# A fused recurrent, retention and feed-forward block: in the gates, weight forms and retention operands are issued behind stated copies, and the last value stages take one PSUM tile per key block

## The chip, the core and the metric

The kernel runs on one core of a Trainium2 chip. The metric is device microseconds of one execution, as the median of several runs. The engines that matter here are TensorE (PE in the profile; its weight loads are PEld), VectorE (DVE), ScalarE (ACT) and SyncE (SP), which issues the loads. Each engine works its own queue in order.

## What is computed

One layer over 528 tokens (16 meta tokens and 512 of the sequence) with model width 1024. After an RMS norm, one large projection gives a recurrent branch (an RG-LRU with its gate, called branch a), a retention branch with four heads (branch b) and a gate for each branch. The two branches are mixed, projected and added; a gated convolutional feed-forward follows.

```python
z = xn @ w_in[l]
u_rnn, u_gate, q, k, v, g_ret, ga, gb = jnp.split(z, IN_SPLITS, axis=-1)
...
o_a = hr * jax.nn.gelu(u_gate)
...
o = retention(q, k, v.reshape(bsz, t, RET_HEADS, RET_DV))
o_b = head_rms(o).reshape(bsz, t, RET_HEADS * RET_DV) * jax.nn.silu(g_ret)
mixed = (jax.nn.sigmoid(ga) * (o_a @ w_branch_rnn[l])
         + jax.nn.sigmoid(gb) * (o_b @ w_branch_ret[l]))
h = h + mixed @ w_out[l]
```

## The kernel before

**Numbers.** Every fp32 matrix is split into a high and a low fp16 piece; a product is three fp16 matmuls (high by high, high by low, low by high). `split` (L91 to L93) makes the pieces: an activation on ScalarE writes the high one, an instruction on VectorE the low one, and reads the high one for it.

**Fast units.** A weight block that is marked `fast` is multiplied with seven half-size products in place of eight. For that the block is formed in five steps (`fast_steps`): B11; B21 with B22; the sums (three VectorE additions in place in the raw tile, L255 to L257); T1 with T3; T4 with T2. The last two steps read what the sums have written. The tokens' forms (A11, A12, F3, F5, F6, F7) are made once.

**Queue of steps.** Weights come by DMA into `raw`, two buffers of 1 MB, and are formed into `wt`, ten buffers. The steps of all units stand in one list in the order of use. `tick` emits the next step if the units in hand take no more than `ahead` tiles; `get` emits what remains of a unit when it is needed. From L716 on the order of the instructions on each engine is not written out by hand: a planner takes the program's order as priority, simulates the engines and issues what is ready, so a step that is late in the program can be issued early. `tc.issue_after(ins)` adds an edge from `ins` to each instruction of the block that runs on the engine of `ins`.

**Gates.** `fast_products` (L839) runs the seven products of a gate unit in the order P1, P7, P6, P2, P5, P3, P4, each of 12 matmuls of 257 columns. P1, P6, P5 and P3 add up in one PSUM bank, `pa`; between them ScalarE copies the bank out (`keep`, L852). P7 and P4 use `pe`, P2 uses `pb`. VectorE adds the kept copies (L869, L873, L880), ScalarE applies the gate's function (L885). `gated` runs the two gate units of a retention head between the output products of the next head (L932). At the end of a unit `ob_forms` makes the second branch's operands from the gated head: four subtractions on VectorE and four splits. `gate_a` takes the gates of branch a, with `branch` (60 matmuls, `pm`) between; the last head's gate units lie among them, and one `u_ga` unit is started before the retention gate ahead of it is finished. `gate_b` takes the gates of branch b and then `mix_products`, the second branch's own fast products, the only reader of the `ob` tiles.

**Values.** `values` (L887) makes the values of one head for five blocks of keys. Four blocks take 24 matmuls of 512 columns, the last 16. Two blocks share a PSUM tile of two banks (`acc`, two tiles in this stage), one bank each; a split follows each block. Heads 2 and 3 have their value stages between the gated heads, near 322 to 345 and 372 to 396 us.

**After the gates** come the output projection, the norm and the up products, where forms of the activations already wait in a list `pending` behind a last copy and a last sum.

## Time and profile before

| | before |
|---|---|
| median of 3 runs | 1069.34 us (1069.12 to 1069.63) |
| profiled execution, own time | 1069.46 us |
| its span | 1067.7 us |
| TensorE busy | 1050.2 us, 98% |
| VectorE busy | 860.5 us, 81% |
| ScalarE busy | 589.7 us, 55% |
| DMA | 111.49 MB, mean 104 GB/s |
| granted TensorE clock, mean | 0.999 |

The span is the stretch that the profiler saw; the own time has 1.8 us more around it. TensorE's busy time has little room above it, and matmuls overlap one another in the rows, so what can be won or lost lies in single gaps of TensorE. They are found in the time line by the idle time in brackets behind an instruction, with the one that ended it. The rows give start, length, engine, line and operation; where several equal instructions follow one another, they are one row with a count.

### The profile page before, as it was taken

To read this page: it belongs to the slowest core of one execution; us is meant where nothing else is said; L and a number is where in the kernel's file an instruction comes from. 1 tells how busy PE (TensorE), PEld (TensorE's weight loads), DVE (VectorE), ACT (ScalarE), POOL (GpSimd) and SP (SyncE) were. 2 spreads that over 40 slices of the span, in tenths; PEclk is the share of its full clock that TensorE was granted. 3 is DMA by queue.
4 is the path that set the end of the run, shared out by engine and by line. 5 is a ranking of instruction groups with operands and counts; after the bars stand their busy time and mean duration, and the time that the engine had idled before them with its cause. 6 is when DMAs were issued, how large, how long until landed. Compare 5 with 4: busy or idle time off the path is not lost.

```text
span 1067.7 us, 21013 instructions
## 1 busy us (share of the span) xinstructions
PE 1050.2 (98%) x8995; PEld 851.5 (80%) x8995; DVE 860.5 (81%) x1289; ACT 589.7 (55%) x927; POOL 6.9 (1%) x20
## 2 busy tenths in 40 slices
PE   9999999999999999999999999999999999999997
PEld 6888888865684848888888886588888888888884
DVE  6885799998786969887787785489789897988975
ACT  7568954434564747466454453475565465454442
POOL 2000000000000000000000000000000000000000
PEclk9999999999999999999999999999999999999999
DMA  8341243431211322333333365042332324214322
GB/s 255 102 133 44 80 139 119 160 120 40 80 41 51 108 65 65 122 95 106 118 105 119 103 214 178 7 153 86 113 107 92 119 81 133 66 60 137 102 80 80
DMA packets 108989, 111.49 MB, mean 104 GB/s; under 512 B 5610, under 2 KB 100560, under 8 KB 108896
## 3 DMA queue, kind: packets, MB, share of 16 engines
q1 hardware_dynamic: 108448, 109.74, 31.9%
q8 instruction: 70, 1.15, 0.4%
q10 hardware_dynamic: 160, 0.27, 0.1%
q0 software_dynamic: 288, 0.14, 0.1%
q14 instruction: 23, 0.19, 0.1%
HBM read 108.04 MB, written 2.10 MB: 103 GB/s over the span
## 4 chain that ended last, share of the span: by engine, by line
PE 74%; DVE 14%; ACT 8%; issue 2%; DMA 1%; ACTq 0%; DVEq 0%
PE ps L398 29%; PE P L1455 9%; PE pa L847 9%; PE pm L398 4%; PE ps L910 4%; DVE wt L93 4%; PE pe L847 4%; PE ps L1183 3%; PE pb L847 2%; PE ps L411 2%; PE pa L1346 2%; ACT wt L92 2%; PE ps L932 1%; DVE rnn L645 1%; PE pe L1346 1%
## 5 line engine op out<-in xcount | busy, mean ns | idle before, releaser
L398 PEld LDWEIGHTS <-wt 128*128 128x128 f16 x3840 | 373.2, 97 | 58.2 <-DVE t L739 1.4
L93 DVE SCALAR_TENSOR_TENSOR wt<-raw,wt 128x1024 f16<-128x1024 f32 (+2 forms) x278 | 303.9, 1105 | 68.9 <-ACT wt L92 67.9
L92 ACT ACTIVATE wt<-raw 128x1024 f16<-128x1024 f32 (+2 forms) x278 | 263.4, 963 | 153.5 <-PE P L1455 25.3
L847 PEld LDWEIGHTS <-wt 128*128 128x128 f16 x2016 | 195.1, 97 | 34.7 <-issue 7.4
L398 PE MATMUL ps<-x2h,wt 128*128 128x258 f16 x1184 | 181.2, 273 | 0.0
L398 PE MATMUL ps<-xh,wt 128*128 128x257 f16 (+2 forms) x1056 | 163.9, 275 | 1.1 <-DVE t L739 1.1
L398 PE MATMUL ps<-x2l,wt 128*128 128x258 f16 x592 | 113.2, 272 | 0.0
L398 PE MATMUL ps<-xl,wt 128*128 128x257 f16 (+2 forms) x528 | 102.2, 275 | 0.0
L1455 PE MATMUL P<-wt,act 128*128 128x256 f16 x792 | 88.3, 273 | 0.0
L1455 PEld LDWEIGHTS <-act 128*128 128x128 f16 x792 | 77.5, 98 | 9.0
L1324 DVE SCALAR_TENSOR_TENSOR cv<-ps,vt,cv 128x512 f32<-128x512 f32 x80 | 59.8, 747 | 26.5 <-ACT cv L1322 25.6
L910 PE MATMUL ps<-wt,xh 128*128 128x512 f16 x256 | 76.1, 379 | 2.3 <-DVE v L93 2.3
L847 PE MATMUL pa<-xs,wt 128*128 128x257 f16 x576 | 71.6, 273 | 3.4 <-ACT kept L852 3.1
L398 PE MATMUL pm<-oa,wt 128*128 128x257 f16 x480 | 55.4, 274 | 0.0
L1322 ACT ACTIVATE cv<-ps,vt,vt 128x512 f32<-128x512 f32 x40 | 31.0, 774 | 38.5 <-PE ps L398 37.9
L910 PEld LDWEIGHTS <-xh 128*128 128x128 f16 x256 | 24.8, 98 | 31.4 <-issue 3.4
L910 PE MATMUL ps<-wt,xl 128*128 128x512 f16 x128 | 48.3, 379 | 0.0
L255 DVE TENSOR_TENSOR raw<-raw 128x1024 f32<-128x1024 f32 x39 | 47.6, 1220 | 0.7
L847 PE MATMUL pa<-ob,wt 128*128 128x257 f16 x384 | 45.7, 274 | 0.6 <-ACT last L852 0.5
L1183 PE MATMUL ps<-wt,mx 128*128 128x512 f16 x192 | 44.3, 378 | 0.0
L1346 PEld LDWEIGHTS <-wt 128*128 128x128 f16 x336 | 32.6, 97 | 4.4
L411 PEld LDWEIGHTS <-wt 128*128 128x128 f16 x288 | 27.9, 97 | 5.8 <-issue 1.3
(290 smaller groups left out, 1406.6 us busy)
## 6 DMA issues: line engine op xcount, KB each, us to landing
raw<-in_w_in SPq DMA_DIRECT2D x40, 1024.0 KB, 4.9
raw<-in_w_up SPq DMA_DIRECT2D x24, 1024.0 KB, 5.2
raw<-in_w_down SPq DMA_DIRECT2D x48, 256.0 KB, 3.4
raw<-in_w_branch_ret SPq DMA_DIRECT2D x16, 512.0 KB, 4.8
raw<-in_w_branch_rnn SPq DMA_DIRECT2D x8, 640.0 KB, 4.5
raw<-in_w_out SPq DMA_DIRECT2D x4, 1024.0 KB, 5.1
xin<-in_x SPq DMA_DIRECT2D x4, 512.0 KB, 5.7
raw<-in_w_in SPq DMA_DIRECT2D x4, 512.0 KB, 8.2
```

Of the source, the lines that this page charges most:

```text
L92: nc.scalar.activation(hi, src, AF.Copy, scale=s)
L93: nc.vector.scalar_tensor_tensor(lo, src, s, hi, op0=ALU.mult, op1=ALU.subtract)
L255: nc.vector.tensor_tensor(pair, pair, rv[:, :, right].rearrange("p (h k) c -> p h k c", h=2), op=ALU.add)
L398: nc.tensor.matmul(ps[:, hf, :n], w(aw, k, col, P), src(ax, k, c0, n), start=k == 0 and (aw, ax) == (0, 0), stop=k == nk - 1 and aw == 1)
L411: mm = nc.tensor.matmul(ps[:, hf, :n], w(aw, k, col, P), src(ax, k, c0, n), start=k == 0 and (aw, ax) == (0, 0), stop=k == KD - 1 and aw == 1)
L847: nc.tensor.matmul(ps[:, :257], ws[k // 4](wf, aw, k % 4), src(xf_, ax, k), start=first and k == 0 and (aw, ax) == (0, 0), stop=k == last_ ...
L910: nc.tensor.matmul(pb, xf(ax, k, XF + j0, nb), w(aw, k % 4, 0, 512), start=i == 0, stop=i == 23)
L1183: nc.tensor.matmul(ps[:, n], mx[k][:, a, c0:c0 + P], wo[k // 2](aw, k % 2, n * 512, 512), start=k == 0 and (a, aw) == (0, 0), stop=k == ks ...
L1322: nc.scalar.activation(vv_, src[:, :, 2:258], AF.Identity, scale=vt2[:, 96 + ch:97 + ch], bias=bias)
L1324: nc.vector.scalar_tensor_tensor(vv_, src[:, :, j:j + 256], vt2[:, 48 * j + ch:48 * j + ch + 1], vv_, op0=ALU.mult, op1=ALU.add)
L1346: nc.tensor.matmul(ps[:, :258], w(wf, aw, k), x2_form(xf_, ax, k), start=first and k == 0 and (aw, ax) == (0, 0), stop=k == 3 and aw == 1, ...
L1455: nc.tensor.matmul(pd[:, 256 * tt:256 * tt + 256], t[:, ax, c0 + tt * P:c0 + tt * P + P], w(wf, aw, i), start=q % 6 == 0 and tt == 0 and i ...
```

## The change

In `fast_steps` the two steps that read the sums are wrapped, so that their instructions on ScalarE may not be issued before the gate copy (`keep`) that was traced last; they carry a mark `late`. `tick` can be told to leave late steps where they are, and the gates tell it so at P1 and P7. The operands of the second branch are no longer made at once at the end of a retention gate unit: `ob_forms` returns three portions, which are put in `pending` and emitted by `flush`, one at each of P7, P6 and P5 of a later gate unit or after a key block of `values`, also behind the last copy. `gating` switches the edge off inside `mix_products`. In `values`, heads 2 and 3 take a PSUM tile for each key block and use its first bank.

```diff
@@ -1,4 +1,4 @@
-from contextlib import ExitStack
+from contextlib import ExitStack, nullcontext
 
 import concourse.bass as bass
 import concourse.tile as tile
@@ -262,11 +262,25 @@
             i, c0 = at[nm]
             return tiles[i][a][:, k, c0:c0 + bc]
 
+        def late(run):
+            def behind():
+                with behind_copy():
+                    run()
+            behind.late = True
+            return behind
+
         wviews.append(form)
         return [cut(top, left), cut(low, slice(0, 2 * bc)), sums,
-                cut(top, slice(0, 2 * bc)), cut(low, slice(0, 2 * bc))]
+                late(cut(top, slice(0, 2 * bc))), late(cut(low, slice(0, 2 * bc)))]
 
     steps = []
+    last_keep = [None]
+    gating = [True]
+
+    def behind_copy():
+
+        return nullcontext() if last_keep[0] is None or not gating[0] else tc.issue_after(last_keep[0])
+
     done = [0]
     ahead = [6]
     current = [0]
@@ -292,7 +306,8 @@
             emit_step()
         return wviews[u]
 
-    def tick(n=1):
+    def tick(n=1, late=True):
+
 
         for _ in range(n):
             if done[0] == len(steps):
@@ -301,6 +316,8 @@
                 queue(unit_load())
             u = steps[done[0]][0]
             if sum(unit_tiles(i) for i in range(current[0], u + 1)) > ahead[0]:
+                return
+            if not late and hasattr(steps[done[0]][1], "late"):
                 return
             emit_step()
 
@@ -849,7 +866,7 @@
                                      skip_group_check=True)
 
         def keep(dst, ps):
-            nc.scalar.activation(dst, ps[:, :257], AF.Copy)
+            last_keep[0] = nc.scalar.activation(dst, ps[:, :257], AF.Copy).ins
 
         kept, last = wtile("kept"), wtile("last")
         g0, g1 = wtile("g0"), wtile("g1")
@@ -888,9 +905,9 @@
         vt = []
         wa, wb = get(u_v[h][0]), get(u_v[h][1])
         for b, (j0, nb) in enumerate(JB):
-            if b % 2 == 0:
+            if h >= 2 or b % 2 == 0:
                 ps = acc("ps")
-            pb = ps[:, b % 2]
+            pb = ps[:, 0 if h >= 2 else b % 2]
             vt.append(piece([P, 2, 512], F16, f"v{h}"))
             i = 0
             if b == 4:
@@ -910,6 +927,7 @@
                     nc.tensor.matmul(pb, xf(ax, k, XF + j0, nb), w(aw, k % 4, 0, 512), start=i == 0, stop=i == 23)
                     i += 1
             split(vt[b][:, 0], vt[b][:, 1], pb, S_V / (SW * S_XN))
+            flush()
             tick()
         vv[h] = vt
 
@@ -957,28 +975,57 @@
         def finish(j, g):
             nc.vector.tensor_mul(ot[2 * i + j], g[:, :TQ], ot[2 * i + j])
             if j == 0:
-                ob_forms(h, i, ot[2 * i], ot[2 * i + 1])
+                pending.extend(ob_forms(h, i, ot[2 * i], ot[2 * i + 1]))
 
         return fast_products([get(u_gr[h][i])], x_forms, gate_func(AF.Silu), finish)
 
     def ob_forms(h, i, t0, t1):
 
         h0, h1 = slice(0, 257), slice(257, TQ)
-        d, y = wtile("d"), wtile("y")
-        nc.vector.tensor_tensor(d[:, h1], t0[:, h1], t1[:, h1], op=ALU.subtract)
-        nc.vector.tensor_tensor(y[:, h0], t0[:, h0], t0[:, h1], op=ALU.subtract)
-        nc.vector.tensor_tensor(d[:, h0], t0[:, h0], d[:, h1], op=ALU.subtract)
-        nc.vector.tensor_tensor(y[:, h1], d[:, h0], t1[:, h0], op=ALU.subtract)
-        if i == 0:
-            ob_a11.append(piece([P, 2, TQ], F16, "ob11"))
-        a11 = ob_a11[h]
-        split(a11[:, 0, 257 * i:257 * i + 257], a11[:, 1, 257 * i:257 * i + 257], t0[:, h0], S_OB)
-        at = {"A11": (a11, 257 * i)}
-        for src, s, nms in ((t1, S_OB, ("A12", "A22")), (y, S_OB, ("F7", "F3")), (d, -S_OB, ("F6", "F5"))):
+        at = {}
+        tmp = {}
+        ob.append(at)
+
+        def differences():
+            d, y = tmp["d"], tmp["y"] = wtile("d"), wtile("y")
+            nc.vector.tensor_tensor(d[:, h1], t0[:, h1], t1[:, h1], op=ALU.subtract)
+            nc.vector.tensor_tensor(y[:, h0], t0[:, h0], t0[:, h1], op=ALU.subtract)
+            nc.vector.tensor_tensor(d[:, h0], t0[:, h0], d[:, h1], op=ALU.subtract)
+            nc.vector.tensor_tensor(y[:, h1], d[:, h0], t1[:, h0], op=ALU.subtract)
+
+        def both(src, s, nms):
             t = piece([P, 2, TQ], F16, "ob")
             split(t[:, 0], t[:, 1], src[:, :TQ], s)
             at.update({nm: (t, 257 * n) for n, nm in enumerate(nms)})
-        ob.append(at)
+
+        def plain():
+            if i == 0:
+                ob_a11.append(piece([P, 2, TQ], F16, "ob11"))
+            a11 = ob_a11[h]
+            split(a11[:, 0, 257 * i:257 * i + 257], a11[:, 1, 257 * i:257 * i + 257], t0[:, h0], S_OB)
+            at["A11"] = (a11, 257 * i)
+            both(t1, S_OB, ("A12", "A22"))
+
+        def formed():
+            both(tmp["y"], S_OB, ("F7", "F3"))
+            both(tmp["d"], -S_OB, ("F6", "F5"))
+
+        return [differences, plain, formed]
+
+    pending = []
+
+    def flush(n=1):
+
+        for _ in range(min(n, len(pending))):
+            with behind_copy():
+                pending.pop(0)()
+
+    def advance(run, *names):
+        for nm in names:
+            next(run)
+            if nm in ("P7", "P6", "P5"):
+                flush()
+            tick(1, nm not in ("P1", "P7"))
 
     def scale_head(h, i):
         for d in (2 * i, 2 * i + 1):
@@ -992,14 +1039,10 @@
             next(a)
             if i == 0:
                 head_norm(h)
-            for _ in range(2):
-                next(a)
-                tick()
+            advance(a, "P7", "P6")
             next(other)
             scale_head(h, i)
-            for _ in range(2):
-                next(a)
-                tick()
+            advance(a, "P2", "P5")
             next(other)
             for _ in a:
                 pass
@@ -1071,11 +1114,6 @@
                                        sig.pop(c).rearrange("p (a b) -> p a b", a=2), op0=ALU.mult, op1=ALU.mult)
         mix_a.append(m)
 
-    def advance(run, n):
-        for _ in range(n):
-            next(run)
-            tick()
-
     def rest(run):
         for _ in run:
             pass
@@ -1084,7 +1122,7 @@
         if run is None:
             run = mix_unit(u_ga, i)
             next(run)
-        advance(run, 4)
+        advance(run, "P7", "P6", "P2", "P5")
         ps = branch(u_ba, oa_of, NR)
         rest(run)
         mix_first(2 * i, ps)
@@ -1095,28 +1133,31 @@
         next(run)
         if i == 0:
             head_norm(3)
-        advance(run, 2)
+        advance(run, "P7", "P6")
         ps = branch(u_ba, oa_of, NR)
         mix_first(2 * i + 1, ps)
         scale_head(3, i)
-        advance(run, 2)
+        advance(run, "P2", "P5")
         after = mix_unit(u_ga, i + 1)
         next(after)
         rest(run)
         gate_a(i + 1, after)
     mix_first(5, branch(u_ba, oa_of, NR))
+    flush(3)
 
     def gate_b(i):
 
         ahead[0] = 10
         run = mix_unit(u_gb, i)
-        advance(run, 3)
+        advance(run, "P1", "P7", "P6")
         ahead[0] = 12
-        advance(run, 2)
+        advance(run, "P2", "P5")
         rest(run)
+        gating[0] = False
         for _ in mix_products(i):
             tick(2)
         tick()
+        gating[0] = True
         ahead[0] = 10
 
     gate_b(0)
```

## Rows read from the trace of the kernel before

**Rows 1.** The page: busy time of each engine, and the chain that ended last.

```profile
PE 1050.2 (98%) x8995; PEld 851.5 (80%) x8995; DVE 860.5 (81%) x1289; ACT 589.7 (55%) x927; POOL 6.9 (1%) x20
...
PE 74%; DVE 14%; ACT 8%; issue 2%; DMA 1%; ACTq 0%; DVEq 0%
```

**Rows 2.** TensorE's waits, 287 to 655 us: total, times, longest.

```profile
PE pa L847 <- ACT kept L852: 3.1, 5, 1.1
PE ps L910 <- DVE v L93: 2.0, 2, 1.4
```

**Rows 3.** Busy time by stretch: length, then busy of each engine, clock, DMA share.

```profile
397.00:422.00 25.00, 24.82 (x249) 21.79 (x248) 24.79 (x37) 18.92 (x34) 0.00 (x0) 1.00 0.31 92
...
750.00:950.00 200.00, 200.00 (x1801) 174.70 (x1800) 167.64 (x247) 109.33 (x160) 0.00 (x0) 1.00 0.30 96
```

**Rows 4.** Time line, TensorE: start, length, line, operation, count [idle before, releaser].

```profile
312.88 0.27 PE L847 MATMUL pb<-xl,wt 128*128 128x257 f16 x1
```

**Rows 5.** Time line, TensorE and ScalarE, around five waits in the gates.

```profile
312.56 1.06 ACT L92 ACTIVATE wt<-raw 128x1024 f16<-128x1024 f32 x1 [0.25 <-DVE raw L255]
313.94 1.49 PE L847 MATMUL pa<-xs,wt 128*128 128x257 f16 x12 [0.78 <-ACT kept L852]
...
429.68 0.61 ACT L92 ACTIVATE ob<-d 128x514 f16<-128x514 f32 x1
430.62 1.49 PE L847 MATMUL pa<-xs,wt 128*128 128x257 f16 x12 [1.06 <-ACT kept L852]
...
474.21 1.06 ACT L92 ACTIVATE wt<-raw 128x1024 f16<-128x1024 f32 x1
475.60 1.49 PE L847 MATMUL pa<-xs,wt 128*128 128x257 f16 x12 [0.17 <-ACT kept L852]
...
544.11 1.06 ACT L92 ACTIVATE wt<-raw 128x1024 f16<-128x1024 f32 x1 [1.90 <-DVE raw L257]
545.08 0.62 ACT L92 ACTIVATE mx<-m 128x514 f16<-128x514 f32 x1
546.02 1.16 PE L847 MATMUL pa<-xs,wt 128*128 128x257 f16 x9 [0.60 <-ACT kept L852]
...
596.26 1.06 ACT L92 ACTIVATE wt<-raw 128x1024 f16<-128x1024 f32 x1 [2.66 <-DVE raw L255]
597.65 1.49 PE L847 MATMUL pa<-xs,wt 128*128 128x257 f16 x12 [0.48 <-ACT kept L852]
```

**Rows 6.** Time line, TensorE, ScalarE and VectorE, in the value stages.

```profile
331.27 0.59 PE L910 MATMUL ps<-wt,xh 128*128 128x512 f16 x2 [0.50 <-DVE v L93]
...
371.59 0.60 PE L910 MATMUL ps<-wt,xh 128*128 128x512 f16 x2
372.02 0.38 PE L910 MATMUL ps<-wt,xl 128*128 128x512 f16 x1
...
379.30 0.63 ACT L92 ACTIVATE ob<-y 128x514 f16<-128x514 f32 x1 [2.40 <-DVE y L971]
381.53 0.68 DVE L93 SCALAR_TENSOR_TENSOR v<-ps,v 128x512 f16<-128x512 f32 x1
382.26 0.59 PE L910 MATMUL ps<-wt,xh 128*128 128x512 f16 x2 [1.45 <-DVE v L93]
```

**Rows 7.** Time line, TensorE, ScalarE and VectorE, around a branch a unit.

```profile
452.62 1.49 PE L847 MATMUL pa<-xs,wt 128*128 128x257 f16 x12
454.15 0.39 ACT L852 ACTIVATE last<-pa 128x257 f32<-128x257 f32 x1 [1.98 <-PE pa L847]
455.50 1.28 ACT L885 ACT_TABLE_LOAD   x1
455.52 1.22 DVE L93 SCALAR_TENSOR_TENSOR wt<-raw,wt 128x1024 f16<-128x1024 f32 x1 [0.48 <-ACT wt L92]
457.93 1.49 PE L847 MATMUL pe<-xs,wt 128*128 128x257 f16 x12
```

**Rows 8.** The page: DMA issues, count, size, median us to landing.

```profile
raw<-in_w_in SPq DMA_DIRECT2D x40, 1024.0 KB, 4.9
```

## Prediction, before the change was run

> **What bounds the kernel now.** I read the page's first part, then the busy time by stage, then TensorE's waits in the gates, then the time lines around each of them. TensorE is busy for 98% of the span and makes up 74% of the chain that ended last [rows 1], so only two things can move the time: TensorE's work, which the change leaves as it is, and the gaps in that work. The reader should look for gaps in the gate stage, from 287 to 655 us. There TensorE waited 3.1 us in five places for a ScalarE copy of a PSUM sum and 2.0 us in two places for the VectorE half of a value split [rows 2]; the few shorter waits of the stage the change does not touch, and I leave them. The later up stage has a fast unit of the same seven products, and its retiring forms are already held behind its last copy and last sum; TensorE was busy there for 200.00 of 200.00 us [rows 3]. That is the nearest picture of what the gates could be.
>
> An idle time in a row is less than what was lost. A matmul of 257 columns lasts 0.27 us [rows 4], and twelve in a row take 1.49 (the row at 313.94 [rows 5]), so they start (1.49 - 0.27) / 11 = 0.11 us apart, and a wait first eats 0.16 us of overlap: a row with [0.78] is a loss of 0.94 us. Two matmuls of 512 columns take 0.60 and one 0.38 [rows 6], so they start 0.22 apart: again 0.16.
>
> **Part 1, forms of the weights behind a stated copy.** Each gate unit has seven products of 12 matmuls. `pa` is used by P1, P6, P5 and P3 in turn; between two of them ScalarE must copy the bank out, with P7, P2 or retention matmuls as the cover. ScalarE works its queue in order, and the planner has put weight forms of the next unit (T1/T3, T4/T2) into that queue early, where they wait for VectorE's sums while a copy that is ready stands behind them. The rows show it four times [rows 5]: the form at 312.56 waited for the sums of L255, and the copy behind it let TensorE start only at 313.94 (loss 0.78 + 0.16 = 0.94); the form at 474.21 stands before the copy awaited at 475.60 (0.33); that at 544.11 waited 1.90 for the sums of L257 (loss at 546.02: 0.76); that at 596.26 waited 2.66 for L255 (loss at 597.65: 0.64). After the change each of these forms is traced behind a copy at least as late as the one that it blocked, and may not be issued before it. Three of the four losses go whole. Of the one at 546.02 only part: the split of `mx` at 545.08 is not gated and can still take its 0.62 us ahead of the copy. Between nothing and 0.76 is won there; I take 0.31, a little under half. So 0.94 + 0.33 + 0.31 + 0.64 = **2.2 us**, bounds 1.9 (the 546.02 place gains nothing) and 2.7.
>
> **Part 2, retention forms behind a copy.** The same row group shows the fifth case: `ob<-d` at 429.68 belongs to the head before, waited (through `ob<-y`) for VectorE's differences and held the copy for which TensorE waited until 430.62: 1.06 + 0.16 = **1.2 us**. After the change these forms come in three portions behind the copies of the next unit's P7, P6 and P5, so none stands ahead of the copy it now blocks. Their work is unchanged: per head half four subtractions, four high pieces and four low ones; nobody needs them before the second branch, a whole stage later. Nothing below zero speaks for an own cost; the bound above is that one portion (two pieces of 0.6 us on ScalarE) stands before a copy again, 1.2 us, which I keep in the range.
>
> **Part 3, a PSUM tile per key block in the last two value stages.** Block 0 of head 3's stage starts at 371.59 [rows 6]; block 1 is another bank of the same tile and starts only when block 0's split is through. The planner lets block 2 go ahead, and breaks it off. TensorE stood until 331.27 in head 2's stage and until 382.26 in head 3's: 0.50 + 1.45 + 2 x 0.16 = **2.3 us**. The split was late because retention forms, again waiting for VectorE (`ob<-y` at 379.30 after 2.40 us), stood in front; these move behind it too. With a tile per block, block 1 takes the second tile, and the wait goes to block 2, which reuses block 0's tile. Two blocks of 24 matmuls take 2 x 24 x 0.22 = 10.5 us, so block 2 starts at 382.1; even with the split as late as now (381.53 + 0.68 = 382.21) it loses 0.1 us. I take 2.2 us, bounds 2.0 and 2.3. The Trainium skill (Perfetto Trace Analysis, Matmul Optimizations) asks that all eight PSUM banks be used; the change leaves the second bank of these tiles empty, two blocks in flight where there were four places. By the rule the wait would stay; this is a rival below.
>
> **What is new.** The ticks at P1 and P7 emit no late form, so a form can be one tick later; where steps remain, the unit's own request emits them at once. The forms cost the same, 1.06 us on ScalarE and 1.22 us on VectorE each, but can no longer be made a unit ahead. Who needs them: P7 wants T3, P6 wants T2. Where a branch (60 matmuls, 6.6 us) or a value stage lies between the last copy and the next unit, that covers them. The tight places are the two units of `u_ga` that are started before the retention gate ahead of them is finished: P5 starts at 452.62, its copy at 454.15, the next unit's P7 at 457.93 [rows 7]. From the end of the copy, 454.54, T3 needs 1.06 + 1.22 and is there at 456.8: 1.1 us early. If the table load of 1.28 us that is at 455.50 and the three gate activations go first, some 2.1 us, T3 is about 1.0 late. I take 0.5 us for each of two such places, and 0.3 for each of three retention heads, where VectorE is fullest (24.79 of 25.00 us in the last of them [rows 3]) and where two lower halves (2.44 us) enter while others leave to the value stage: **1.9 us**, bounds 0 and 6.1 (that is 1.22, one lower half late, at five places).
>
> **Queues.** No moved step issues a DMA of its own, but a `raw` tile comes free only when its forms are made, and the load of the unit after next stands behind that on SP. A load of 1 MB lands in 4.9 us [rows 8]; a gate unit of 84 matmuls alone takes 84 x 0.11 = 9.2 us. Forms that come up to a unit later leave that cover thin but standing; I cost it at nothing, and at up to 1 us in the range. GpSimd has nothing here.
>
> **Sum.** 2.2 + 1.2 + 2.2 - 1.9 = 3.7 us less. The stages behind the gates run TensorE nearly without a gap, so I carry it through. The profiled execution took 1069.46 us (span 1067.7); the median of the runs is 0.12 below it. 1069.34 - 3.7 = **1065.6 us**, by this case's own bounds 1062.9 (2.7 + 1.2 + 2.3 = 6.2 won, and 0.2 for waits too short to show) to 1067.2 (2.1 won).
>
> **Rivals.** *One blocked copy for another*: the gates' forms still wait for sums, now in front of the next copy or gate activation, and only the value stages pay. VectorE's load in the heads speaks for it, the clean up stage against it. Value stages 2.2 won, gates 3.4 won and 4.5 lost: 1068.2. This is also the case in which the statement does little, because it orders ScalarE's instructions alone and the sums on VectorE come when they come.
>
> *Slower*: each of 15 gate units after the first has two late forms behind one copy and before the next. The five losses now seen average 0.78 us. If such a block appeared in 12 units it would cost 9.4, less 5.6 won: 1073.1. It decides against the change from 10 units on (7.8 - 5.6 = 2.2). For it: forms in advance are cover, and this change gives cover away in every unit. Against: most units have a branch or retention matmuls in between.
>
> *The banks*: the value wait only moves to block 2 and stays its old size: 3.7 - 2.2 = 1.5 less, 1067.8. The 10.5 us of matmuls against a split of 1.3 speak against it.
>
> **How the numbers follow.** Forecast 0.62; one copy for another 0.19; slower 0.13; banks 0.06. A difference of 0.2%, 2.1 us, is about what a measurement of this kernel can tell from no change. The forecast gives faster, 0.62; the first and third rival lie within, 0.25; slower 0.13. The range goes from 1062.6, all bounds won, to 1070.6, which takes in all 6.1 us of late forms against 5.6 won (1069.8) with the load's 1 us nearly whole on top, and leaves out the slower case and little else.
>
> **What would show it.** In the profile after: no idle at a `pa` matmul behind a copy that a `wt` or `ob` form held (else parts 1 and 2 are wrong); no wait of L910 for `v` in the last two value stages, and blocks in their order (else part 3). New idle at `pe<-xs` or at a weight load in the gates, with a `wt` split as its releaser, would show the forms too late; idle at `pa` with VectorE's adds behind a lower half would show the first rival. The prediction is wrong if TensorE's idle in the gates is gone and the time is not, for then a later stage took it back.

## The result, and the profile after

| | before | after |
|---|---|---|
| median | 1069.34 us | 1071.75 us |
| ratio, 95% interval | | 1.0025 (1.0018 to 1.0032) |
| profiled execution, own time | 1069.46 us | 1070.83 us |
| its span | 1067.7 us | 1069.1 us |

The change made the kernel 2.4 us slower. A time 3.7 us shorter had been forecast, and 1071.75 lies outside the range. The line numbers move with the edit: the gate products are now L864 (L847 before), `keep` L869 (L852), the values L927 (L910), the branch L415 (L398).

The page of the changed kernel, the two lines that answer to [rows 1]: busy time of each engine, and the chain that ended last.

```profile
PE 1050.4 (98%) x8995; PEld 850.5 (80%) x8995; DVE 861.0 (81%) x1289; ACT 586.7 (55%) x927; POOL 6.9 (1%) x20
...
PE 76%; DVE 12%; ACT 6%; DMA 3%; issue 2%; ACTq 0%; DVEq 0%
```

The work is the same; in the chain DMA has 3% in place of 1%, and VectorE 12% in place of 14%. TensorE's waits in the gates, 287 to 660 us, which answer to [rows 2] (engine, tile and line, releaser: total, times, longest; a wait of 0.2 us for `ssum`, which every run has, is left out here and below):

```profile
PE pa L864 <- ACT kept L869: 3.1, 4, 1.5
PE pa L864 <- ACT last L869: 2.1, 2, 1.8
PE pa L864 <- DVE wt L93: 1.7, 4, 0.4
```

The value wait (2.0 us before) is gone as forecast. The waits for a copy, which were to go, stand at 5.2 us in six places. Before they were 3.6 us in six: the 3.1 of [rows 2], and 0.5 us for `last` at 644.11, which those rows leave out. Four waits for the lower half of a weight form are new.

**Where the time went.** I set the starts of TensorE's matmuls of both kernels against each other at equal work, that is behind the same number of matmul columns. The difference (minus: the changed kernel is ahead) changes only at single places, so each place has its price. "Order of blocks" means that the same matmuls come in another order there:

| us in the trace of before | what | price | difference after it |
|---|---|---|---|
| 314 | blocked copy gone | -0.91 | -0.95 |
| 316 | not followed further | -0.21 | -1.16 |
| 331 | value wait gone | -0.66 | -1.82 |
| 332 to 355 | order of blocks, not followed further | -0.47 | -2.29 |
| 382 | value wait gone | -1.61 | -3.82 |
| 383 to 400 | order of blocks, not followed further | -0.60 | -4.42 |
| 412 | new blocked copy (408.31 in after) | +0.60 | -3.82 |
| 430 | blocked copy gone | -1.14 | -4.96 |
| 442 | new blocked copy (438.90 us in the trace of after) | +0.59 | -4.37 |
| 476 | blocked copy larger, 0.88 for 0.33 (471.79 in after) | +0.55 | -3.81 |
| 515 to 650 | four lower halves late, 0.85 each | +3.4 | |
| 545 | new blocked copy, 1.66; old one, 0.76, gone | +0.90 | |
| 597 | blocked copy gone | -0.64 | |
| 550 to 650 | short waits | +0.3 | |
| 645 | copy before the last products later, 1.99 for 0.63 | +1.36 | +1.53 |

So by 432 us the change had won 5 us, more than forecast for that stretch. It gave 1.1 back by 480 us, and in the second branch's stage, 515 to 650 us, it lost 5.3 more. Nothing of size happens behind that, and the profiled execution ends 1.37 us later.

The largest new blocked copy. Time line of the changed kernel, ScalarE and TensorE (start, length, engine, line, operation, count, [idle before, releaser]):

```profile
539.47 0.63 ACT L92 ACTIVATE wt<-raw 128x512 f16<-128x512 f32 x1 [2.61 <-DMA raw<-in_w_in]
540.01 1.04 ACT L92 ACTIVATE wt<-raw 128x1024 f16<-128x1024 f32 x1
540.96 0.37 ACT L869 ACTIVATE kept<-pa 128x257 f32<-128x257 f32 x1
541.37 1.49 PE L864 MATMUL pa<-xs,wt 128*128 128x257 f16 x12 [1.50 <-ACT kept L869]
...
643.30 2.00 ACT L92 ACTIVATE wt<-raw 128x1024 f16<-128x1024 f32 x2 [3.95 <-DMA raw<-in_w_out]
645.22 0.37 ACT L869 ACTIVATE last<-pa 128x257 f32<-128x257 f32 x1
645.63 2.82 PE L864 MATMUL pa<-ob,wt 128*128 128x257 f16 x24 [1.83 <-ACT last L869]
```

It is the picture of [rows 5], a copy that is ready behind a form that waits, but the form now waits for a **load** and not for sums: it is the first form of a block, to which the change adds no edge. ScalarE stands for 2.61 us at the head of its queue, then does two forms, and only then the copy. The same happens at 643.30. The load awaited at 539.47 was issued at 532.47, 2.7 us later than before (529.79), and took 6.9 us in place of the 4.9 of [rows 8].

The blocked copies of the heads at 442 and 476 us have another cause. Changed kernel, VectorE, ScalarE and TensorE:

```profile
466.56 3.90 DVE L93 SCALAR_TENSOR_TENSOR wt<-raw,wt 128x1024 f16<-128x1024 f32 x4
470.38 0.42 DVE L897 TENSOR_TENSOR g<-pe,kept 128x257 f32<-128x257 f32 x1
470.83 0.63 ACT L902 ACTIVATE g<-g 128x514 f32<-128x514 f32 x1 [1.57 <-DVE g L897]
471.37 0.37 ACT L869 ACTIVATE kept<-pa 128x257 f32<-128x257 f32 x1
471.79 1.49 PE L864 MATMUL pa<-xs,wt 128*128 128x257 f16 x12 [0.72 <-ACT kept L869]
```

The copy stands behind a gate activation, which waits for VectorE's add, which stands behind four lower halves of weight forms. At 438.90 it is the same, behind three lower halves. This is the sign that the prediction gave for its first rival. At 408.31 three weight forms stand in front, and none of them waits.

ScalarE's waits for loads of these weights, 287 to 660 us, before:

```profile
ACT wt L92 <- DMA raw<-in_w_out: 4.5, 2, 3.4
ACT wt L92 <- DMA raw<-in_w_in: 2.0, 2, 1.7
```

and after:

```profile
ACT wt L92 <- DMA raw<-in_w_in: 13.9, 11, 3.2
ACT wt L92 <- DMA raw<-in_w_out: 5.1, 4, 3.9
```

That is 19.0 us in place of 6.5. The total alone explains nothing, as a run below shows; what counts is whether a copy stands behind such a wait.

One of the four late lower halves, in the changed kernel's second branch products:

```profile
525.57 1.27 PE L864 MATMUL pa<-ob,wt 128*128 128x257 f16 x10 [0.43 <-DVE wt L93]
```

### The profile page after: what moved, and what is told of

Read it like the earlier page. It is cut to its first block, busy times and chain, and to the rows that moved or that the text cites. A ratio compares the mean times of both kernels' runs of the same rounds, so it can differ in the third digit from the quotient of the medians.

```text
span 1069.1 us, 20956 instructions
## 1 busy us (share of the span) xinstructions
PE 1050.4 (98%) x8995; PEld 850.5 (80%) x8995; DVE 861.0 (81%) x1289; ACT 586.7 (55%) x927; POOL 6.9 (1%) x20
## 3 DMA queue, kind: packets, MB, share of 16 engines
q8 instruction: 70, 1.15, 0.4%
## 4 chain that ended last, share of the span: by engine, by line
PE 76%; DVE 12%; ACT 6%; DMA 3%; issue 2%; ACTq 0%; DVEq 0%
PE ps L415 31%; PE P L1496 9%; PE pa L864 7%; PE ps L927 6%; PE pm L415 4%; DVE wt L93 4%; PE pe L864 3%; PE ps L1224 3%; ACT wt L92 2%; PE ps L950 2%; PE ps L428 2%; PE pa L1387 2%; PE pb L864 2%; DMA raw<-in_w_in 2%; DVE rnn L662 1%
## 5 line engine op out<-in xcount | busy, mean ns | idle before, releaser
L415 PEld LDWEIGHTS <-wt 128*128 128x128 f16 x3840 | 373.2, 97 | 58.2 <-DVE t L756 1.4
L92 ACT ACTIVATE wt<-raw 128x1024 f16<-128x1024 f32 (+2 forms) x278 | 260.3, 961 | 128.1 <-DMA raw<-in_w_in 31.7
L864 PEld LDWEIGHTS <-wt 128*128 128x128 f16 x2016 | 194.1, 97 | 40.1 <-issue 8.5
L415 PE MATMUL ps<-x2h,wt 128*128 128x258 f16 x1184 | 181.2, 273 | 0.0
L415 PE MATMUL ps<-xh,wt 128*128 128x257 f16 (+2 forms) x1056 | 163.8, 275 | 1.1 <-DVE t L756 1.1
L415 PE MATMUL ps<-x2l,wt 128*128 128x258 f16 x592 | 113.2, 272 | 0.0
L415 PE MATMUL ps<-xl,wt 128*128 128x257 f16 (+2 forms) x528 | 102.2, 275 | 0.0
L927 PE MATMUL ps<-wt,xh 128*128 128x512 f16 x256 | 76.1, 379 | 0.3 <-DVE v L93 0.3
L864 PE MATMUL pa<-xs,wt 128*128 128x257 f16 x576 | 71.6, 273 | 3.3 <-ACT kept L869 3.1
L415 PE MATMUL pm<-oa,wt 128*128 128x257 f16 x480 | 55.1, 274 | 0.0
L864 PE MATMUL pa<-ob,wt 128*128 128x257 f16 x384 | 46.6, 274 | 3.9 <-ACT last L869 2.1
L927 PE MATMUL ps<-wt,xl 128*128 128x512 f16 x128 | 48.5, 379 | 0.0
L927 PEld LDWEIGHTS <-xh 128*128 128x128 f16 x256 | 24.8, 98 | 29.3 <-issue 0.7
L255 DVE TENSOR_TENSOR raw<-raw 128x1024 f32<-128x1024 f32 x39 | 47.6, 1221 | 0.7
```

Of the source, the lines that this page charges most:

```text
L92: nc.scalar.activation(hi, src, AF.Copy, scale=s)
L255: nc.vector.tensor_tensor(pair, pair, rv[:, :, right].rearrange("p (h k) c -> p h k c", h=2), op=ALU.add)
L415: nc.tensor.matmul(ps[:, hf, :n], w(aw, k, col, P), src(ax, k, c0, n), start=k == 0 and (aw, ax) == (0, 0), stop=k == nk - 1 and aw == 1)
L864: nc.tensor.matmul(ps[:, :257], ws[k // 4](wf, aw, k % 4), src(xf_, ax, k), start=first and k == 0 and (aw, ax) == (0, 0), stop=k == last_ ...
L927: nc.tensor.matmul(pb, xf(ax, k, XF + j0, nb), w(aw, k % 4, 0, 512), start=i == 0, stop=i == 23)
```

## Experiments

There were two explanations at the start. T1 is that the loss is the price of the edge on weight forms: it makes the T forms (the last two of a block) late and keeps the `raw` tiles, and so the loads, back. The other, called the planner below, is that the planner sets the program anew after any edit, and each part moves blocked copies about whatever it is meant to do. The expectations number their theories by themselves. In the first eight runs theory 1 is T1, theory 2 says that the edge inside the second branch's gates makes its own forms late, and theory 3 that the moved retention forms crowd VectorE. In the last four runs each expectation says what its theories are. "Ahead" below is the difference as in the table.

**The value tiles alone**, on the kernel before:

```diff
-            if b % 2 == 0:
+            if h >= 2 or b % 2 == 0:
                 ps = acc("ps")
-            pb = ps[:, b % 2]
+            pb = ps[:, 0 if h >= 2 else b % 2]
```

> The kernel before with the value tiles alone (a PSUM tile per key block for heads 2 and 3). Every theory here takes part 3 to be sound: the two waits of L910 for v go (2.3 us), 1067.1. If a later stage takes it back: 1069.3.

Measured 1072.93 us, ratio 1.0032 (1.0020 to 1.0044), above both figures of the expectation. The value waits are gone, yet TensorE waits 7.6 us for `kept` in nine places and 2.4 for `last` in three. The first of them:

```profile
362.62 0.94 ACT L92 ACTIVATE ob<-or 128x257 f16<-128x257 f32 x2 [1.71 <-DVE or L958]
363.81 1.06 ACT L92 ACTIVATE wt<-raw 128x1024 f16<-128x1024 f32 x1 [0.25 <-DVE raw L255]
364.77 0.37 ACT L852 ACTIVATE kept<-pa 128x257 f32<-128x257 f32 x1
365.19 1.04 PE L847 MATMUL pa<-xs,wt 128*128 128x257 f16 x8 [1.48 <-ACT kept L852]
```

Retention and weight forms stand before the copy. The part wins its 2.3 us and loses 5.9 elsewhere: its price can't be read from the places it touches.

**All but the edge on weight forms**, from the changed kernel:

```diff
-                late(cut(top, slice(0, 2 * bc))), late(cut(low, slice(0, 2 * bc)))]
+                cut(top, slice(0, 2 * bc)), cut(low, slice(0, 2 * bc))]
```

> The changed kernel without the edge and the held ticks on the weight forms: value tiles and retention forms in three portions behind a copy stay. Theory 1 (held weight forms keep raw tiles, loads come late, forms wait for data in ScalarE's queue): no load is late, 1069.3 - 2.2 - 1.2 = 1065.9. Theory 3 (the moved retention forms crowd VectorE): the loss of the second branch stays, 1069 to 1071.

Measured 1067.5 us, 0.9984 (0.9976 to 0.9993): halfway between the two theories in time. Theory 3 falls, for all but 0.3 us of the second branch's loss is gone. TensorE is 4.9 us ahead at 450 us, 0.5 of it from before 100 us; with the edge it is 4.4. So in the heads the edge won nothing that shows. What is missing against T1 is one place:

```profile
451.67 0.63 ACT L92 ACTIVATE wt<-raw 128x512 f16<-128x512 f32 x1 [7.63 <-DMA raw<-in_w_in]
452.21 0.37 ACT L869 ACTIVATE last<-pa 128x257 f32<-128x257 f32 x1
452.63 2.58 PE L864 MATMUL pa<-xs,wt 128*128 128x257 f16 x12 [2.08 <-ACT last L869]
```

Again a first form that waits for its load before a copy, and here without any edge on weight forms. The load is not late: it goes out at 444.74 us, as in the kernel before (444.15), but takes 6.8 us to land in place of 4.9, and the form is early in the queue. Why it takes longer wasn't followed. ScalarE's waits for loads add up to as much as with the edge:

```profile
ACT wt L92 <- DMA raw<-in_w_in: 14.4, 5, 7.6
ACT wt L92 <- DMA raw<-in_w_out: 5.2, 2, 3.5
```

So T1's "no load is late" doesn't hold as a sum of waits; what the edge decides is where the waits fall. The place costs 3.9 us, more than its 2.24 of wait, because the next twelve matmuls take 2.58 us and not 1.49; the last section comes back to this. The loads themselves show what the edge does to them. SP's time line of this kernel:

```profile
282.03 88.73 SPq L103 DMA_DIRECT2D raw<-in_w_in  x8
...
410.87 0.37 SPq L103 DMA_DIRECT2D raw<-in_w_in  x1
...
428.05 0.37 SPq L103 DMA_DIRECT2D raw<-in_w_in  x1
```

and of the changed kernel:

```profile
310.07 70.12 SPq L103 DMA_DIRECT2D raw<-in_w_in  x8
...
420.98 0.37 SPq L103 DMA_DIRECT2D raw<-in_w_in  x1
...
436.13 0.37 SPq L103 DMA_DIRECT2D raw<-in_w_in  x1
```

The only difference between the two kernels is the edge with its held ticks, and the same loads go out 28, 10 and 8 us later. By the second branch less of that is left: the loads awaited at 539.47 and 643.30 in the changed kernel go out 3.4 and 5.6 us later.

**The edge on weight forms alone**, values and retention forms as before:

```diff
-                pending.extend(ob_forms(h, i, ot[2 * i], ot[2 * i + 1]))
+                for part in ob_forms(h, i, ot[2 * i], ot[2 * i + 1]):
+                    part()
```

(and the value tiles' lines undone)

> The weight forms behind stated copies alone, with value tiles and retention forms as before. Theory 1: 2.2 us won in the gates, some 5.9 lost behind them, 1073.0, with the spread of the changed kernel. Theory 3: 1069.3 - 2.2 = 1067.1 with little spread.

Measured 1077.91 us, 1.0081 (1.0069 to 1.0094). This is T1's direction, with more than its size; theory 3 falls again. 3.9 us of it is one place near 650 us:

```profile
650.63 4.47 PE L864 MATMUL pa<-ob,wt 128*128 128x257 f16 x24 [2.67 <-ACT last L869]
```

Without the other parts the edge costs 8.6 us, with them 4.2 (1071.75 less 1067.5). T1 and the planner are both needed: the edge does harm, and how much depends on what the planner does around it.

**No edge in the second branch's gates**, from the changed kernel:

```diff
     def gate_b(i):
 
+        gating[0] = False
         ahead[0] = 10
         run = mix_unit(u_gb, i)
-        advance(run, "P1", "P7", "P6")
+        for _ in range(3):
+            next(run)
+            tick()
         ahead[0] = 12
-        advance(run, "P2", "P5")
+        for _ in range(2):
+            next(run)
+            tick()
         rest(run)
-        gating[0] = False
```

> The changed kernel with the edge and the held ticks switched off in the gates of branch b, on everywhere else. Theory 1: the loads are late before branch b begins, so most of the loss stays, 1069.5 to 1072. Theory 2 (the edge inside branch b's gates makes its own forms late): the gain at 510 us stays, 1065.5 to 1066.5.

Measured 1069.0 us, 0.9998 (0.9990 to 1.0007), between the two ranges and nearer to T1's. The four waits for lower halves are gone, so they are the edge's doing in these gates. Copies behind forms that wait for sums come back in their place:

```profile
507.77 1.06 ACT L92 ACTIVATE wt<-raw 128x1024 f16<-128x1024 f32 x1 [2.78 <-DVE raw L255]
509.28 2.52 ACT L92 ACTIVATE wt<-raw 128x1024 f16<-128x1024 f32 x3 [0.46 <-DVE raw L257]
511.71 0.37 ACT L869 ACTIVATE kept<-pa 128x257 f32<-128x257 f32 x1
512.12 1.05 PE L864 MATMUL pa<-xs,wt 128*128 128x257 f16 x8 [1.83 <-ACT kept L869]
```

The load of the unit ahead of them goes out at 489.78 us, like the changed kernel's at 490.13 and not like that of before at 482.16, since the edge still holds the heads' loads back. Whether that is the root of these two places is the question of a run below.

**The changed kernel with three staging buffers.** Memory for the third comes from two other pools:

```diff
-    pieces = ctx.enter_context(tc.tile_pool(name="pieces", bufs=46))
-    wraw = ctx.enter_context(tc.tile_pool(name="wraw", bufs=2))
-    wsp = ctx.enter_context(tc.tile_pool(name="wsp", bufs=10))
+    pieces = ctx.enter_context(tc.tile_pool(name="pieces", bufs=44))
+    wraw = ctx.enter_context(tc.tile_pool(name="wraw", bufs=3))
+    wsp = ctx.enter_context(tc.tile_pool(name="wsp", bufs=9))
```

> The changed kernel with three raw buffers in place of two; to make room, 44 piece buffers in place of 46 and nine weight tiles in place of ten. Theory 1 (a raw tile held by its late forms delays the load of the unit after next, and forms then wait for data in front of copies): the loads need not wait, the copies at 541 and 645 us are free and the lower halves in time: 1065 to 1066.5. Theory 2 (the edge in branch b's gates by itself makes the forms late): 1069 to 1072, waits at the same places.

Measured 1071.11 us, 1.0012 (1.0002 to 1.0021), in theory two's range and no faster than the control below; the profiled execution took 1069.42. Its waits in the gates:

```profile
PE pa L864 <- DVE wt L93: 1.7, 4, 0.4
PE pa L864 <- ACT kept L869: 0.7, 2, 0.4
PE pa L864 <- ACT last L869: 0.5, 1, 0.5
```

ScalarE waits 0.7 us for loads in place of 19.0, the blocked copies shrink from 5.2 us to 1.2, and TensorE is 2.31 us ahead at 650 us where the changed kernel is 1.53 behind: 3.8 us between them. The lower halves stay as they were. So in the profile the loads and the lower halves are two separate causes: the loads' part of T1 holds for the first, theory two for the second. The median shows nothing of this gain. The norm near 702 us waits behind three weight forms on VectorE (TensorE idle for 2.55 us there, 1.44 in the control) and gives 1.4 back, and seven of the ten executions are some 1.7 us longer than the profiled one (last section). The time shows the gain in a later run, with the edge out of the second branch's gates.

**The control: the two smaller pools alone**, with two staging buffers as before.

> Control: the changed kernel with 44 pieces and nine weight tiles and two raw buffers as before. Both theories: about the changed kernel, 1071 to 1073.

Measured 1070.76 us, 1.0016 (1.0006 to 1.0026), a little below the expectation. The waits are as in the changed kernel (`last` 3.2, `kept` 2.3, lower halves 1.7): what the third buffer did to the waits was not the smaller pools' doing.

**Three buffers without the edge on weight forms** (both edits above):

> The kernel without the weight forms' edge (value tiles and moved retention forms stay), with three raw buffers, 44 pieces, nine weight tiles. Its one large loss was a form that waited 7.6 us for its load in front of a copy near 452. Theory 1: that goes, 1067.5 - 3.9 = 1063.6. Theory 2: as without, 1067 to 1068.

Measured 1067.27 us, 0.9982 (0.9972 to 0.9991), 3.7 more than T1's figure and in theory two's range. The loss at 452 us is gone, but TensorE loses about 1.6 us more before 305 us and 2.17 at a new place, where a form waits 1.81 us for the sums of L255 before a copy.

**The kernel before with the same three pools:**

> The kernel before with three raw buffers, 44 pieces, nine weight tiles. Its blocked copies wait for sums and differences, not for loads: both theories 1068.5 to 1070.

Measured 1071.13 us, 1.0016 (1.0007 to 1.0026), 1.1 us above the range expected. The third buffer does nothing for the kernel before, whose copies don't stand behind loads, and the new pools cost it 1.6 us before 305 us (the control above had no such loss, so it isn't the smaller two alone).

**The retention forms alone**, on the kernel before (in portions behind copies; no edge on weight forms, shared value tiles):

> The kernel before with the retention forms alone put into portions behind the copies; values in shared tiles and weight forms as before. Theory one, each part brings its own saving: the blocked copy at 430 us goes and nothing else moves, 1.2 us less, 1068.1 us, TensorE 1.1 to 1.2 us ahead of the kernel before from 440 us on, the value waits of 2.0 us still there. Theory two, effects that simply add, read off the two runs made so far (values alone 3.6 us more, values with retention forms 1.8 us less): retention forms alone 5.4 us less, 1063.9 us. Theory three, the planner sets the forms anew and a form that waits stands before some other copy: between 1067 and 1073 us, with at least one wait of TensorE for a copy, at a place where the kernel before has none, behind a form that waited over 1 us.

Measured 1067.67 us, 0.9985 (0.9975 to 0.9994). Theory one is the nearest, with 1.6 us less for the 1.2 expected. All of TensorE's waits of over 0.4 us from 287 to 660 us:

```profile
328.61 0.59 PE L927 MATMUL ps<-wt,xh 128*128 128x512 f16 x2 [1.29 <-DVE v L93]
...
379.04 0.59 PE L927 MATMUL ps<-wt,xh 128*128 128x512 f16 x2 [1.05 <-DVE v L93]
...
544.19 1.49 PE L864 MATMUL pa<-xs,wt 128*128 128x257 f16 x12 [0.61 <-ACT kept L869]
...
595.83 1.49 PE L864 MATMUL pa<-xs,wt 128*128 128x257 f16 x12 [0.48 <-ACT kept L869]
...
642.28 2.82 PE L864 MATMUL pa<-ob,wt 128*128 128x257 f16 x24 [0.47 <-ACT last L869]
```

The copies of [rows 5] at 314 us and 430 us are free (TensorE ahead by 1.15 and another 1.0), the second of them by design, the first with no edge on any weight form. Why the first goes, the trace of before shows, just ahead of the form at 312.56:

```profile
311.36 0.94 ACT L92 ACTIVATE ob<-or 128x257 f16<-128x257 f32 x2 [1.71 <-DVE or L958]
```

That form itself waited 0.25 us; what held ScalarE up were retention forms. One value wait grows by 0.8 us, the other shrinks by 0.4. The blocked copies at 544 and 596 us stay, and from 432 us on the difference rests at 1.82. This part alone has no loss behind it.

**No edge in the second branch's gates, and three buffers:**

> The changed kernel without the edge on weight forms in the second branch's gates, with three staging buffers for weights in place of two, 44 pieces and 9 weight tiles in place of 46 and 10. The smaller pools cost 1.6 us before 290 us in the kernel before. Theory one, the two blocked copies near 512 and 561 us of the run with two buffers (3.0 us) have late loads as their root, the sums being late because the load was: they go, 1069.0 + 1.6 - 3.0 = 1067.6 us. Theory two, they are late because VectorE comes to the sums late, whatever the load: they stay, 1070.6 us, and the forms in front of the copies still wait over 2 us for the sums.

Measured **1065.34 us, 0.9964 (0.9951 to 0.9977)**, the best of all. Its waits in the gates:

```profile
PE pa L864 <- ACT kept L869: 1.3, 3, 0.6
PE pa L864 <- ACT last L869: 0.5, 1, 0.5
```

It is 3.7 us faster than the same kernel with two buffers and the old pools (1069.0; the smaller pools alone were tried only with the edge in place, where the median moved by 1.0). Theory one holds: the blocked copies near 512 and 561 us are gone. The unit's load goes out at 485.89 us in place of 489.78 and those sums begin at 504.72 in place of 506.51. A form still waits 2.29 us for them, but before the copy is due, and TensorE loses nothing. It is 4.95 us ahead at 432 us and still 4.63 at 650. The 1.6 us that the new pools cost the kernel before don't appear here, which is most of the 2.3 us by which the run beat the expectation.

**The first form of a block behind the copy**, to cure the place at 452 us, from the kernel without the edge on T forms (no tick is held):

```diff
-        return [cut(top, left), cut(low, slice(0, 2 * bc)), sums,
+        return [late(cut(top, left)), cut(low, slice(0, 2 * bc)), sums,
```

> Values and retention forms as in the changed kernel; of the five steps of a weight block only the first, whose form waits for the load, stands behind the last copy, and no step is held at a product. Theory one, the 3.9 us lost at 452 us in the run without any edge on weight forms come from that form standing before the copy, and the edge cures it: 1067.5 - 3.9 = 1063.6 us if all goes, 1065.3 if only the 2.2 us of the wait named goes, with TensorE 4 to 5 us ahead at 480 us. Theory two, the edge makes first forms late, buffers come free later and the loads behind them too: a form that waits for a load or sums stands before another copy, 1067 to 1070 us.

Measured 1075.0 us, 1.0052 (1.0035 to 1.0068). This is theory two in kind, 5 us above its range in size. The place at 452 us falls to 0.50, but first forms come late, and the largest loss is the old pattern with the load of another weight:

```profile
646.11 2.00 ACT L92 ACTIVATE wt<-raw 128x1024 f16<-128x1024 f32 x2 [4.95 <-DMA raw<-in_w_out]
648.02 0.37 ACT L868 ACTIVATE last<-pa 128x257 f32<-128x257 f32 x1
648.44 4.24 PE L863 MATMUL pa<-ob,wt 128*128 128x257 f16 x24 [3.17 <-ACT last L868]
```

**The best version with shared value tiles:**

> The kernel of the run without the edge in the second branch's gates and with three staging buffers, its values of the last two heads back in shared PSUM tiles. Theory one, the tile per block is worth its 2.0 to 2.3 us there as forecast: 1065.34 + 2.2 = 1067.5 us, the value waits of 2.0 us back, and the wait for copies in the gates under 2.5 us as now. Theory two, the planner sets the forms anew as it did when the values alone were changed, and the time says nothing on the tiles: outside 1066.8 to 1068.2 us, with a wait of TensorE over 1 us at a copy that has none now, behind a form that waited.

Measured 1069.15 us, 0.9999 (0.9990 to 1.0009): 3.8 us more than with a tile per block, outside theory one's range, yet without the new blocked copy of theory two: the waits for copies are the same three and one. The price lies in the value stages:

```profile
329.77 0.59 PE L927 MATMUL ps<-wt,xh 128*128 128x512 f16 x2 [1.33 <-DVE v L93]
...
380.43 0.59 PE L927 MATMUL ps<-wt,xh 128*128 128x512 f16 x2 [1.32 <-DVE v L93]
```

Two waits, 2 x (1.33 + 0.16) = 3.0 us, and 0.9 from the order of blocks inside the stages.

## Why the prediction was wrong

**The waits named and their prices: right.** By 432 us the four places forecast for that stretch had gone at 0.91, 0.66, 1.61 and 1.14 us where 0.94, 0.66, 1.61 and 1.22 stood in the working. In the second branch the two at 546 and 597 us went at 0.76 and 0.64 (0.31 and 0.64 taken). Only the copy awaited at 475.60 stayed blocked, and worse.

**Part 1, the edge on weight forms: wrong in whom it credits.** The first of its losses, 0.94 us, goes in the runs with retention forms alone and without any edge on weight forms. The row in [rows 5] was misread: the form at 312.56 waited 0.25 us, and the retention forms in front of it had waited 1.71. The form at 474.21 has no wait in its row at all. Without the edge TensorE is as far ahead at 450 us as with it. What the edge really won were the two places in the second branch, 1.4 us, and it cost 4.2 net, 1071.75 against 1067.5, although the loss of 3.9 us at 452 us is found only without it.

**Part 2: right** (1.2 forecast at its place, 1.0 to 1.1 found; the part alone gives 1.6).

**Part 3: right at its places, mis-sized as a part.** The waits went at 2.3 us. Alone the part makes the kernel 3.6 us slower, and in the best version it is worth 3.8. The wait didn't move to block 2, as the 10.5 us of cover said, so the third rival falls. The Trainium skill's rule (Perfetto Trace Analysis, Matmul Optimizations) to use all eight banks does not decide here: with the second bank of these tiles empty TensorE has no value wait left.

**What is new, the term of 1.9 us: right within its bounds, wrong in its place.** I put it on the paired `u_ga` units and the retention heads; neither shows a wait of TensorE for a late form, though at 442 and 476 us the lower halves hold a copy up by way of VectorE's add. It came as four lower halves in the second branch's products, 4 x 0.85 = 3.4 us. I had passed these by since the edge is off inside them; but their first forms are made in the gate unit ahead, where it is on. Taking it off there removes them.

**Queues, "I cost it at nothing, and at up to 1 us in the range": the step that failed.** I compared the 4.9 us of a load with the 9.2 us of a unit and called the cover standing. The cover was used up elsewhere: forms that come late hold both `raw` tiles, the `w_in` loads of the heads go out 8 to 28 us later than without the edge, those that the two places below wait for 3.4 and 5.6 us later, and the first form of the next block, which waits for the load, goes to the head of ScalarE's queue before a copy. At the two places of the time line that is 1.66 + 1.36 = 3.0 us. With a third buffer both are gone, about half of what is lost at 442 and 476 us with them, and TensorE is 3.8 us further ahead at 650 us. I had asked whether TensorE would wait for a load. It never does by name; it waits for a copy behind a form behind a load.

**The rivals.** "One blocked copy for another" is what 412, 442 and 476 us show, 1.74 us in all for the 4.5 of that rival, a figure for which it gave no working. At two of the three the copy waits as that rival had it, behind a gate activation for which VectorE's add comes late. "Slower" (1073.1) had the right sign and the nearest time, but its mechanism, a block in ten or more units, did not occur: six waits for copies in the whole stage. The slower result came from three terms that the sum held too small, not from that: the loads (3.0 us, taken at nothing), the late lower halves (3.4, taken at 1.9) and the newly blocked copies of the heads (1.7, taken at nothing). The places named won 5.7 us for the 5.6 forecast, and the order of blocks, with the place at 316 us, another 1.3 that I had not forecast. With 0.3 of short waits that makes 3.0 + 3.4 + 1.7 + 0.3 - 5.7 - 1.3 = 1.4 us, which is what the profiled execution shows.

With the first two taken away, by no edge in the second branch's gates and a third buffer, the kernel takes 1065.34 us. That the sum's 1065.6 lies near this is luck: the term for late forms is gone there, and some blocked copies remain.

**Slips in the working.** The bound of 1067.2 is no sum of the lower bounds: 1.9 + 0 + 2.0 less 6.1 would be a loss. It is the 2.1 us that the prediction calls the least that can be told from no change. The 1062.6 of the range stands 0.3 below the 1062.9 of the same bounds. Neither decides anything here.

**Open:** why the changed kernel's runs spread from 1070.54 to 1075.31 us; a possible cause is in the last section. The profiled execution explains 1.37 us of the 2.41 between the medians.

## What to carry to other kernels

An edge that holds work back holds its input buffers back too: follow it to the load that reuses the buffer, and to whoever stands first in line for that load. An in-order queue makes every instruction that can wait, for sums, differences or a load, a possible block before a copy that another engine needs; ordering one kind of them leaves the others, so the number to watch is the releaser of what stands just ahead of the copy. And where a planner orders the program, price an edit by taking parts away from the whole, not by its own places: one part here, the value tiles, made the kernel 3.6 us slower alone and 3.8 us faster in company.

## What the runs showed of the hardware

**A wait can cost more than its length, through TensorE's clock.** Granted clock by stretch in the kernel without the edge on weight forms, around its 2.08 us of idle time (length, busy of each engine with counts, then the clock):

```profile
448.00:452.60 4.60, 2.54 (x23) 2.09 (x22) 1.79 (x4) 0.93 (x3) 0.00 (x0) 1.00 0.82 235
452.60:456.00 3.40, 3.37 (x17) 2.44 (x17) 3.33 (x5) 3.37 (x6) 0.00 (x0) 0.53 0.01 3
```

In the stretch behind the wait the clock is at 0.53, almost all of it at the lower level of 1.2 GHz, and twelve matmuls take 2.58 us in place of 1.49; in the next 4 us it is at 0.97. Behind 2.67 us in the kernel with the edge alone (clock 0.66 from 650 to 655 us) and 3.17 in the one with first forms behind the copy (0.64 from 648.4 to 652.6), 24 matmuls took 4.47 and 4.24 us in place of 2.82 (the changed kernel's row at 645.63, behind 1.83 of idle time). It doesn't always happen: with three buffers and no edge 2.01 us was followed by twelve matmuls in 1.49 us at a clock of 1.00, and the 2.55 us in the changed kernel with three buffers by a clock of 1.00.

**That fits the spread in two kernels.** Of the changed kernel's executions with three buffers, the three with a mean clock of 0.998, the profiled one among them, took 1069.39 to 1069.55 us, and the seven with 0.996 or 0.997 took 1070.9 to 1071.4: some 1.7 us apart. Of the executions of the kernel without the edge, the five with a mean clock of 0.999 took 1067.05 to 1067.57 us (the four with 0.998 1067.15 to 1067.98) and the two with 0.997 took 1068.67 (the profiled one) and 1068.93: 1.6 us apart, as much as the low stretch cost in the profile (3.9 - 2.24 = 1.7). The changed kernel has a wait of 1.83 us, and its longest execution, 1075.31, a mean clock of 0.996. But its executions at 0.999 already reach from 1070.54 to 1072.00, and those at 0.998 from 1070.64 to 1073.37, so the clock, at the three digits that are on record, doesn't explain all of the spread. No trace of a long execution of it was taken, so for the changed kernel this is argued and not shown. The best version, with no wait above 0.63 us in the gates, stays within 1065.19 to 1065.56.
